# Token-major products 512 columns wide in a two-layer hybrid decoder

## The chip, the cores and the metric

The kernel runs on one core of a Trainium2 chip. The metric is the device time of one execution, in microseconds. Three executions of the kernel before took 2058.93, 2059.01 and 2060.22 us; the median is 2059.01 us.

A core has a matrix engine (TensorE, PE in the profile, with its weight loads as PEld), a vector engine (VectorE, DVE), an engine for pointwise functions (ScalarE, ACT), GpSimd (POOL) and SyncE (SP), which issues DMAs here. TensorE multiplies a stationary operand, loaded ahead, with a moving operand that streams through, and writes to PSUM, where DVE and ACT read it. PSUM is used as eight tiles of 128 partitions by 512 float32 numbers.

## What is computed

Two layers of a decoder over 512 tokens of width 1024, batch 1. Each layer normalizes x, multiplies it by one wide matrix `w_in` and feeds four branches: a short gated convolution, a sparse attention (an indexer scores all earlier tokens, each token attends to its 128 best), a gated linear recurrence over chunks of 64 tokens (HGRN2), and a cross-attention into 256 memory tokens. Each branch is lifted to width 1024, gated, summed and projected; then comes a gated feed-forward block of width 2816.

```python
h = rmsnorm(x, norm_mix)
(a_x, a_b, a_c, d_q, d_k, d_v, i_q, i_k, i_w,
 g_q, g_f, g_i, g_g, m_q, gate_logits) = split_cols(h @ w_in)
y_a = a_b * causal_conv3(a_c * a_x, conv_w)
y_b = dsa_attention(q, k, d_v, iq, ik, iw)       # q, k normed per head; q, k, iq, ik rotated
y_c = rmsnorm(hgrn2_chunkwise(hq, hk, hv, log_f)) * silu(g_g)
y_m = softmax(mq @ mk.T) @ mv                    # mk, mv = split(rmsnorm(mem) @ mem_w_kv)
merged = sum(gates[n] * (branches[n] @ w_lift[n]) for n in range(4))
x = x + merged @ w_out
gate, up = split(rmsnorm(x, norm_ffn) @ ffn_w_up)
x = x + (silu(gate) * up) @ ffn_w_down
```

All of it is float32.

## The kernel before

**Products.** Every large product is made of three matmuls (`mm3`, lines 260 to 262): both operands are split into a high part, rounded to the engine's faster float32 type, and a low remainder, and hi x hi, hi x lo and lo x hi are summed in PSUM. Weights are loaded by `wchunk` (class `Chunk`, line 216 for the DMA, on SP) into `w_raw`, 2048 columns at most, two buffers. ACT copies a part of up to 1024 columns into `w_hi` and DVE subtracts it to give `w_lo` (line 225); of these parts there are three buffers. Both are given a high priority.

Two kinds of products stand on this.

- `features` (line 242) gives a feature-major result: the stationary operand is a 128x128 tile of the weights, the moving one is 512 tokens of the activations. Each matmul is 512 wide. Two such results are in work at a time. Most of the kernel is of this kind.
- `tokens` (line 252) gives a token-major result: the stationary operand is a 128-token tile of the activations, the moving one the weights' columns. A chunk has 256 columns (in one case 200), so each matmul is 256 wide. One token tile is finished over all contraction steps before the next is begun.

`tokens` is used at four places: `mem_kv` (line 417), keys and values of the memory for both layers, at the start; `values` (line 657), the recurrence's values; `projections` (line 820), q, k, v and the indexer's iq, ik, iw of the sparse attention; and `final` (line 1012), the last part of the second layer's down projection, which ends the kernel.

**Projections.** Five chunks, each with a handler that empties the accumulator of a token tile: `c_kv` (k, v, two heads of iq), `c_iq` (four heads of iq), `c_last` (two heads of iq, ik, iw) and `c_q` twice (four heads of q each). A handler copies a group of heads into a tile `unit` (three buffers; k and ik go into `twin`, two buffers), norms q and k per head (`headnorm`), rotates (`rope`), transposes on PE into a PSUM tile `tr` (line 744) and splits the result into qS or iqS (ACT and, line 751, DVE).

**PSUM.** The eight tiles are divided among `mm` (results of `features` and `tokens`, `MM_BUFS` = 3), `tr` (transpositions and small sums, `TR_BUFS` = 3) and `at` (attention scores and the like, `AT_BUFS` = 2).

**Order.** The program is written with generators. A string `EARLY` per layer says in which order steps of the projections (b), the convolution (c), the memory attention (m) and the selection of the 128 best (s, `select`, on DVE) are emitted. Then `lift` of the memory branch is woven with the rest of the selection, and `lift` of the convolution and `values` with `attend`; then comes the recurrence (its logits zf, zq, zg, line 870, and `head`), lifts, the output projection and the feed-forward block. On top of this a planner with a simulated timeline reorders the instructions of each engine: it takes by priority (order of emission, but for what was given a high one) what its model holds ready, so matmuls of different steps interleave. At run time each engine keeps that order.

```python
for c0, n, handle in ((C_DK, 256, c_kv), (C_DK + 256, 256, c_iq), (C_DK + 512, 200, c_last),
                      (C_DQ, 256, c_q(0)), (C_DQ + 256, 256, c_q(1))):
    w = wchunk(w_in[l][:, c0:c0 + n], KD, n)
    for t in range(NT):
        ps = mm_ps()[:, :n]
        tokens(w, h, t, ps)
        handle(ps, t)
    yield
```

Of the kernel before, what the change touches and what calls it, by code (L numbers as in the profile page):

```python
# [12 lines left out]
F32 = mybir.dt.float32  # L13
# [8 lines left out]
P = 128  # L22
# [22 lines left out]
EARLY = ["mmbcmmbmmbsccsmmcsssmsccbmb", "mmbmmbmmcbsccsmmcsssmsccbmb"]  # L45
MM_BUFS = 3
TR_BUFS = 3
# [22 lines left out]
def hybrid_trunk(ctx: ExitStack, tc: tile.TileContext, x, mem, positions, norm_mix, w_in, conv_w,  # L70
# [171 lines left out]
    def features(w, a, js, k0=0, kt=None, pss=None):  # L242
        """Feature-major products of the 128-column tiles js of a chunk."""
# [8 lines left out]
    def tokens(w, a, t, ps, k0=0, kt=None):  # L252
        kt = w.kt if kt is None else kt
        for k in range(k0, k0 + w.kt):
            mm3(ps, pair(a, k, slice(t * P, (t + 1) * P)), w.at(k - k0), k == 0, k == kt - 1)
# [114 lines left out]
    mem_r2, mem_r4 = small(4, name="mem_r2", bufs=1), small(4, name="mem_r4", bufs=1)  # L370

    def mem_in_T():
# [10 lines left out]
        dve.tensor_copy(mem_r4.rearrange("p (a b) -> p a b", b=2), mem_r[:, :, None].to_broadcast([P, 2, 2]))  # L383
        dve.tensor_mul(mem_r2, mem_r4, mem_r4)
# [32 lines left out]
    def mem_kv(l):  # L417
        kv = sp.tile([P, 4, 2, 2, MEM], F32R, name="kv", bufs=1)
        for q in range(2):
            w = wchunk(mem_w_kv[l][:, q * 256:(q + 1) * 256], KD, 256)  # L420
            kus = []
            ms, r = small(4), small(4, "mk_r", 2)
            for t in range(2):
                ps = mm_ps()[:, :256]
                tokens(w, mt, t, ps)
                ku = sp.tile([P, 2, P], F32, name="ku", bufs=3)
                with tc.high_priority(offset=AHEAD):
                    A(ku.rearrange("p a b -> p (a b)"), ps, AF.Copy)
                for j in range(2):
                    sq = sp.tile([P, P], F32, name="mk_sq", bufs=2)  # L430
                    A(sq, ku[:, j, :], AF.Square, scale=P ** -0.5, accum_out=ms[:, 2 * t + j:2 * t + j + 1])
                kus.append(ku)
            dve.tensor_mul(ms, ms, mem_r2)
            rstd_into(r, ms, small, 4)
            dve.tensor_mul(r, r, mem_r4)
            for t in range(2):
                for j in range(2):
                    dve.tensor_scalar(kus[t][:, j, :], kus[t][:, j, :], r[:, 2 * t + j:2 * t + j + 1], None, op0=OP.mult)
            for j in range(2):
                ps = tr_ps()[:, :MEM]  # L440
                for t in range(2):
                    pe.transpose(ps[:, t * P:(t + 1) * P], kus[t][:, j, :], ident)
# [662 lines left out]
```

## Time and profile before

| | |
|---|---|
| Median of three executions | 2059.01 us |
| Span of the profiled execution | 2057.1 us |
| Instructions | 27077, of which 10588 matmuls |
| PE busy | 2046.8 us |
| PEld, DVE, ACT busy | 1731.1, 1270.5, 1017.1 us |
| DMA, mean over the span | 99 GB/s |
| 512-wide matmuls of mm3 (three lines of 2320) | 6960 |
| 256- and 200-wide token-major matmuls | 2016 and 192 |

The span goes from the first to the last of the program's own instructions in the profiled execution; the executions that are timed have no profile, and their median is 1.9 us above that span. Times in the profile are microseconds unless marked ns, and a line L260 is line 260 of the kernel. In the table of groups a row reads: line, engine, operation, written tile <- read tiles, shape, count, busy time, mean duration, and idle time of the engine before it. In the timeline the first number is the start and the second the duration (of all `xN` if several are merged), and a bracket at the end gives the engine's idle time before the instruction and what ended it. Durations of matmuls include their latency and overlap; the distance between two starts is what a matmul costs the engine. In a tile's or a line's view a row gives shortest, median and longest duration in ns, then the first and the last start.

### The profile page before, as it was taken

Reading aid. Unit: us, or ns where it says so; the run is one execution under the profiler, and the core shown is the slowest. Engines: PE = TensorE matmul, PEld = TensorE weight load, DVE = VectorE, ACT = ScalarE, POOL = GpSimd, SP = SyncE. Lnnn points to the kernel's source line nnn. Section 1 sums busy time; section 2 is a strip of 40 time slices with the busy share of each in tenths; the row PEclk is TensorE's granted clock in tenths of the full one; section 3 lists DMA queues with packets and bytes.
Section 4 is the critical chain, followed back from the end, with each engine's and each line's share of the span. In section 5 each row is a group of like instructions: output and inputs, shape, how many; then the busy total and the mean of one; then the engine's idle time right before and its main releaser. Section 6 shows DMA issues by size and latency. Waiting matters only on the chain.

```text
span 2057.1 us, 27077 instructions
## 1 busy us (share of the span) xinstructions
PE 2046.8 (99%) x10588; PEld 1731.1 (84%) x10588; DVE 1270.5 (62%) x2513; ACT 1017.1 (49%) x1836; POOL 9.8 (0%) x33
## 2 busy tenths in 40 slices
PE   8999999999999999999999999999999999999999
PEld 8998988888888888888889898888888888888889
DVE  6779998547676544334457899953766754532542
ACT  7654655856665423223355456576657643322321
POOL 0000000000000000000000000000000000000000
PEclk9999999999999999999999999999999999999999
DMA  7632222212233232232242223321223332322322
GB/s 255 215 95 86 72 89 93 81 53 92 82 113 113 83 102 92 92 114 92 87 154 93 88 75 97 97 66 62 83 82 109 116 102 83 103 93 92 103 72 93
DMA packets 190783, 203.83 MB, mean 99 GB/s; under 512 B 4270, under 2 KB 182528, under 8 KB 190528
## 3 DMA queue, kind: packets, MB, share of 16 engines
q1 hardware_dynamic: 186944, 193.56, 29.2%
q10 hardware_dynamic: 3552, 8.41, 1.1%
q8 instruction: 83, 1.36, 0.3%
q14 instruction: 44, 0.36, 0.1%
q0 software_dynamic: 160, 0.13, 0.0%
HBM read 191.60 MB, written 10.49 MB: 98 GB/s over the span
## 4 chain that ended last, share of the span: by engine, by line
PE 98%; DMA 1%; DVE 0%; ACT 0%; SPq 0%; issue 0%; DVEq 0%; ACTq 0%
PE mm L261 30%; PE mm L260 30%; PE mm L262 30%; PE tr L705 1%; PE tr L699 1%; PE at L676 1%; PE at L675 1%; PE at L927 1%; DMA w_raw<-in_mem_w_kv_dram 1%; PE at L928 0%; PE at L260 0%; PE at L262 0%; PE at L261 0%; PE at L952 0%; PE tr L643 0%; PE tr L744 0%
## 5 line engine op out<-in xcount | busy, mean ns | idle before, releaser
L261 PE MATMUL mm<-h_lo,w_hi 128*128 128x512 f32 x1664 | 652.1, 392 | 0.0
L260 PE MATMUL mm<-h_hi,w_hi 128*128 128x512 f32 x1664 | 651.8, 392 | 0.0
L262 PE MATMUL mm<-h_hi,w_lo 128*128 128x512 f32 x1664 | 649.5, 391 | 0.0
L225 DVE TENSOR_TENSOR w_lo<-w_raw,w_hi 128x1024 fp32r<-128x1024 f32 (+1 forms) x348 | 419.7, 1207 | 350.7 <-ACT w_hi L97 349.5
L97 ACT ACTIVATE w_hi<-w_raw 128x1024 fp32r<-128x1024 f32 (+1 forms) x348 | 363.5, 1046 | 469.6 <-PE mm L261 416.8
L261 PEld LDWEIGHTS mm<-h_lo,w_hi 128*128 128x128 f32 x1664 | 312.6, 188 | 64.9 <-issue 2.5
L262 PEld LDWEIGHTS mm<-h_hi,w_lo 128*128 128x128 f32 x1664 | 312.4, 188 | 65.1 <-issue 1.4
L260 PEld LDWEIGHTS mm<-h_hi,w_hi 128*128 128x128 f32 x1664 | 312.6, 188 | 64.5 <-issue 2.0
L262 PE MATMUL mm<-w_hi,h_lo 128*128 128x256 f32 (+1 forms) x448 | 128.0, 286 | 0.0
L261 PE MATMUL mm<-w_lo,h_hi 128*128 128x256 f32 (+1 forms) x448 | 126.8, 284 | 0.0
L260 PE MATMUL mm<-w_hi,h_hi 128*128 128x256 f32 (+1 forms) x448 | 126.8, 285 | 0.0
L261 PE MATMUL mm<-a_lo,w_hi 128*128 128x512 f32 x272 | 106.1, 390 | 0.0
L260 PE MATMUL mm<-a_hi,w_hi 128*128 128x512 f32 x272 | 105.9, 389 | 0.0
L262 PE MATMUL mm<-a_hi,w_lo 128*128 128x512 f32 x272 | 105.6, 390 | 0.0
L260 PE MATMUL mm<-y_hi,w_hi 128*128 128x512 f32 x256 | 101.3, 397 | 0.0
L262 PE MATMUL mm<-y_hi,w_lo 128*128 128x512 f32 x256 | 100.2, 392 | 0.0
L261 PE MATMUL mm<-y_lo,w_hi 128*128 128x512 f32 x256 | 100.1, 391 | 0.0
L262 PEld LDWEIGHTS mm<-w_hi,h_lo 128*128 128x128 f32 x448 | 85.6, 191 | 1.4 <-issue 0.8
L260 PEld LDWEIGHTS mm<-w_hi,h_hi 128*128 128x128 f32 x448 | 85.2, 191 | 1.2 <-issue 0.8
L261 PEld LDWEIGHTS mm<-w_lo,h_hi 128*128 128x128 f32 x448 | 85.5, 191 | 0.6
L97 ACT ACTIVATE a_hi<-fg 128x512 fp32r<-128x512 f32 x44 | 27.8, 633 | 109.0 <-DVE fg L1054 109.0
L97 ACT ACTIVATE prob<-prob,small 128x128 f32<-128x128 f32 (+3 forms) x128 | 69.2, 555 | 15.2 <-DVE small L688 14.6
(351 smaller groups left out, 3048.6 us busy)
## 6 DMA issues: line engine op xcount, KB each, us to landing
w_raw<-in_w_in_dram SPq DMA_DIRECT2D x72, 1024.0 KB, 5.0
w_raw<-in_ffn_w_up_dram SPq DMA_DIRECT2D x44, 1024.0 KB, 5.1
w_raw<-in_w_lift_dram SPq DMA_DIRECT2D x32, 512.0 KB, 3.4
w_raw<-in_ffn_w_down_dram SPq DMA_DIRECT2D x16, 1024.0 KB, 5.0
w_raw<-in_mem_w_kv_dram SPq DMA_DIRECT2D x8, 1024.0 KB, 5.2
w_raw<-in_w_out_dram SPq DMA_DIRECT2D x8, 1024.0 KB, 4.9
kv<-kv ACTq DMA_DIRECT2D x8, 512.0 KB, 7.4
xT<-x_spill SPq DMA_DIRECT2D x16, 256.0 KB, 5.8
```

The costliest lines, as they stand in the source:

```text
L97: i = act.activation(dst, src, func, **kw)
L225: dve.tensor_sub(lo, raw[:, k:e], f(hi))
L260: pe.matmul(ps, ah, bh, start=first, stop=False)
L261: pe.matmul(ps, ah, bl, start=False, stop=False)
L262: pe.matmul(ps, al, bh, start=False, stop=last)
L675: pe.matmul(ps, q[:, hh, s], k[0][:, :n], start=True, stop=False)
L676: pe.matmul(ps, q[:, hh, s], k[1][:, :n], start=False, stop=True)
L699: pe.transpose(pp[:, (2 * e + i) * P:(2 * e + i + 1) * P], probs[2 * i + e][:, b * P:(b + 1) * P], ident)
L705: pe.matmul(pv[e * HD:(e + 1) * HD, :], vt[:, b, :], pt[:, b, e * 2 * P:(e + 1) * 2 * P], start=b == 0, stop=b == t)
L927: pe.matmul(pa[:, s], z[:, s], cmr[:, s], start=True, stop=True)
```

## The change

All four places that used `tokens` now use `tokens_wide`. It takes a list of weight chunks that follow one another in the contraction (`halves` makes two chunks of 512 rows each), and a list of accumulators, one per token tile. It goes through the parts of the weights, and for each part through all token tiles, so that a part is used up at once and all accumulators (four; two for the memory) stay open until the last part.

- `mem_kv`: the keys of all four heads in one step of 512 columns, the values likewise; the norms of the keys are made for eight columns at once; two stores to DRAM of all heads in place of four of two heads.
- `values`: one step of 512 columns in place of two of 256.
- `projections`: three chunks of 512, 328 and 384 columns. `c_low` has two heads of q, k, v and four heads of iq; `c_last` four heads of iq, ik and iw; `c_q` six heads of q, in groups of four and two. `EARLY` loses two b's per layer.
- `final`: two steps of 512 columns in place of four of 256; in the last step the add and the store are made in two halves per token tile.
- PSUM: `MM_BUFS` 3 to 4, `TR_BUFS` 3 to 2.

```diff
-EARLY = ["mmbcmmbmmbsccsmmcsssmsccbmb", "mmbmmbmmcbsccsmmcsssmsccbmb"]
-MM_BUFS = 3
-TR_BUFS = 3
+EARLY = ["mmbcmmmmbsccsmmcsssmsccmb", "mmbmmmmcbsccsmmcsssmsccmb"]
+MM_BUFS = 4
+TR_BUFS = 2
...
-    def tokens(w, a, t, ps, k0=0, kt=None):
-        kt = w.kt if kt is None else kt
-        for k in range(k0, k0 + w.kt):
-            mm3(ps, pair(a, k, slice(t * P, (t + 1) * P)), w.at(k - k0), k == 0, k == kt - 1)
+    def tokens_wide(ws, a, kt, pss):
+        k0 = 0
+        for w in ws:
+            for ks, _, _ in w.parts:
+                for t, ps in enumerate(pss):
+                    for k in ks:
+                        mm3(ps, pair(a, k0 + k, slice(t * P, (t + 1) * P)), w.at(k), k0 + k == 0, k0 + k == kt - 1)
+            k0 += w.kt
+    def halves(src, n):
+        return [wchunk(src[i * D // 2:(i + 1) * D // 2], KD // 2, n) for i in range(2)]
...
         def values(hv):
-            for q in range(2):
-                w = wchunk(w_in[l][:, C_GI + q * 256:C_GI + (q + 1) * 256], KD, 256)
-                for t in range(NT):
-                    ps = mm_ps()[:, :256]
-                    tokens(w, h, t, ps)
-                    A(hv[:, t, q * 256:(q + 1) * 256], ps, AF.Copy, scale=r_t[:, t:t + 1])
-                yield
+            pss = [mm_ps() for _ in range(NT)]
+            tokens_wide(halves(w_in[l][:, C_GI:C_GI + 512], 512), h, KD, pss)
+            for t, ps in enumerate(pss):
+                A(hv[:, t, :], ps, AF.Copy, scale=r_t[:, t:t + 1])
+            yield
...
+                def q_part(ps, t, c0, heads, h0):
+                    u = unit(ps, t, c0, heads)
+                    headnorm(u, heads, gq_b[l])
+                    rope(u, heads, t)
+                    heads_T(qS, h0, u.rearrange("p a b -> p (a b)"), heads, t)
+                def c_low(ps, t):
+                    A(vt[:, t, :], ps[:, 192:256], AF.Copy, scale=r_t[:, t:t + 1])
+                    twin(ps, t, 128, True, kS)
+                    iq_part(ps, t, 256, 0)
+                    q_part(ps, t, 0, 2, 6)
                 def c_last(ps, t):
-                    A(iw[:, t, :], ps[:, 192:200], AF.Copy, scale=r8_t[:, t:t + 1])
-                    iq_part(ps, t, 0, 2, 6)
-                    twin(ps, t, 128, False, ikS)
+                    A(iw[:, t, :], ps[:, 320:328], AF.Copy, scale=r8_t[:, t:t + 1])
+                    iq_part(ps, t, 0, 4)
+                    twin(ps, t, 256, False, ikS)
+                def c_q(ps, t):
+                    q_part(ps, t, 0, 4, 0)
+                    q_part(ps, t, 256, 2, 4)
...
-                    for c0, n, handle in ((C_DK, 256, c_kv), (C_DK + 256, 256, c_iq), (C_DK + 512, 200, c_last),
-                                          (C_DQ, 256, c_q(0)), (C_DQ + 256, 256, c_q(1))):
-                        w = wchunk(w_in[l][:, c0:c0 + n], KD, n)
-                        for t in range(NT):
-                            ps = mm_ps()[:, :n]
-                            tokens(w, h, t, ps)
+                    for c0, n, handle in ((C_DQ + 384, 512, c_low), (C_IQ + 256, 328, c_last), (C_DQ, 384, c_q)):
+                        pss = [mm_ps()[:, :n] for _ in range(NT)]
+                        tokens_wide(halves(w_in[l][:, c0:c0 + n], n), h, KD, pss)
+                        for t, ps in enumerate(pss):
                             handle(ps, t)
                         yield
...
     def final(x_tok, w2d, a, kt):
-        for m0 in range(0, KD, 2):
-            cols = slice(m0 * P, (m0 + 2) * P)
-            ws = [(k0, wchunk(w2d[k0 * P:min(k0 + 8, kt) * P, cols], min(8, kt - k0), 256)) for k0 in range(0, kt, 8)]
-            for t in range(NT):
-                ps = mm_ps()[:, :256]
-                for k0, w in ws:
-                    tokens(w, a, t, ps, k0, kt)
-                dve.tensor_add(x_tok[:, t, cols], x_tok[:, t, cols], ps)
+        for m0 in range(0, D, 512):
+            cols = slice(m0, m0 + 512)
+            ws = [wchunk(w2d[k0 * P:min(k0 + 4, kt) * P, cols], min(4, kt - k0), 512) for k0 in range(0, kt, 4)]
+            pss = [mm_ps() for _ in range(NT)]
+            tokens_wide(ws, a, kt, pss)
+            for t, ps in enumerate(pss):
+                for c in ([cols] if m0 == 0 else [slice(m0 + e, m0 + e + 256) for e in (0, 256)]):
+                    dve.tensor_add(x_tok[:, t, c], x_tok[:, t, c], ps[:, c.start - m0:c.stop - m0])
```

104 lines of the change are left out of this document (46 added, 58 removed).

## The prediction

> **What bounds the kernel now.** I read the page first: busy shares, slices and the chain that ended last.
>
> ```profile
> PE 2046.8 (99%) x10588; PEld 1731.1 (84%) x10588; DVE 1270.5 (62%) x2513; ACT 1017.1 (49%) x1836; POOL 9.8 (0%) x33
> PE   8999999999999999999999999999999999999999
> DVE  6779998547676544334457899953766754532542
> PEclk9999999999999999999999999999999999999999
> PE 98%; DMA 1%; DVE 0%; ACT 0%; SPq 0%; issue 0%; DVEq 0%; ACTq 0%
> ```
>
> TensorE (PE) is busy in every slice, at full granted clock, and 98% of the chain is its own work. A busy PE need not be at its peak, so the question is whether it waits between matmuls. The table of waits, for PE alone, answers that. Columns: total us, times, longest.
>
> ```profile
> PE tr L160 <- DMA rows<-in_mem_k_norm_dram: 1.9, 1, 1.9
> PE mm L261 <- DVE w_lo L225: 1.3, 2, 0.8
> ```
>
> These are the longest, 3.2 us, and by the slices PE is below nine tenths in the first alone. For some 2040 us it is handed work without a break, so the time is the sum of what its instructions cost back to back. A change pays if it shortens that sum and opens no holes.
>
> **What one matmul costs.** Durations of matmuls overlap in this profile (each is drawn with its latency). The price of one is the distance between starts, in the timeline.
>
> ```profile
> 1984.74 0.39 PE L262 MATMUL mm<-h_hi,w_lo 128*128 128x512 f32 x1
> ...
> 1985.87 0.39 PE L261 MATMUL mm<-h_lo,w_hi 128*128 128x512 f32 x1
> ...
> 1994.48 0.28 PE L260 MATMUL mm<-w_hi,a_hi 128*128 128x256 f32 x1
> ...
> 1996.40 0.28 PE L261 MATMUL mm<-w_lo,a_hi 128*128 128x256 f32 x1
> ```
> ```profile
> 139.05 0.27 PE L260 MATMUL mm<-w_hi,h_hi 128*128 128x200 f32 x1
> ...
> 139.94 0.27 PE L262 MATMUL mm<-w_hi,h_lo 128*128 128x200 f32 x1
> ```
> ```profile
> 218.20 0.34 PE L675 MATMUL at<-ik_hi,iqS 128*128 128x384 f32 x1
> ...
> 218.55 0.28 PE L261 MATMUL mm<-w_lo,h_hi 128*128 128x256 f32 x1
> ```
>
> 512 wide: 5 steps in 1.13 us, 226 to 227 ns. 256 wide: 16 steps in 1.92 us, 120 ns. 200 wide: 8 steps in 0.89 us, 111 to 112 ns. 384 wide: two of them (L675, L676) in 0.35 us, 175 ns. Two 256s cost 240 ns and one 512 costs 227: 13 ns saved per pair. The 200-wide matmul costs nearly as much as a 256, so it is the worst bargain of all.
>
> **The change, part by part.** How many narrow matmuls there are, from the groups kept apart by shape (one line of mm3 each; two more lines with the same count stand beside every one):
>
> ```profile
> L262 PE MATMUL mm<-w_hi,h_lo 128*128 128x256 f32 x384 | 110.1, 287 | 0.0
> L261 PE MATMUL mm<-w_lo,a_hi 128*128 128x256 f32 x160 | 45.1, 285 | 0.1
> L261 PE MATMUL mm<-w_lo,mt_hi 128*128 128x256 f32 x128 | 37.1, 292 | 1.3 <-DVE w_lo L225 1.3
> L262 PE MATMUL mm<-w_hi,h_lo 128*128 128x200 f32 x64 | 17.9, 280 | 0.0
> ```
>
> Three lines each: 1152 + 480 + 384 = 2016 of width 256 and 192 of width 200. At 120 and 112 ns that is 241.9 + 21.5 = 263.4 us.
>
> After: memory keys and values 384 become 192 of 512; values() 384 become 192 of 512; final() 480 become 240 of 512. The projections, 96 matmuls per chunk and layer, become 192 each of 512, 328 and 384 over two layers. In all 816 of 512 (227 ns, 185.2 us), 192 of 384 (175 ns, 33.6 us) and 192 of 328. No row shows 328: it lies between 256 (120) and 384 (175), and 72/128 of the way is 151 ns, 29.0 us (ends 23.0 and 33.6). Sum 247.8 us. **PE work falls by 15.6 us** (11 to 22 with those ends), of which projections give 7.4, final 3.1, memory and values 2.5 each. The transposes stay: five units and two twins per token tile become five units and two twins.
>
> *Weight parts.* A part of w_hi/w_lo is still 1024 columns or less. Now it holds two contraction steps that all four token tiles use, then is dropped, where before both parts of a chunk were held until the last token tile. In final() that hold made PE wait at each column boundary; the chain of waits shows one of three:
>
> ```profile
> 2006.97 1.07 ACT w_hi L97
> 2008.06 1.24 DVE w_lo L225
> ```
>
> A part lasts 24 x 227 = 5.4 us and takes 1.07 + 1.24 us to split, with three buffers, so this wait goes. What it cost:
>
> ```profile
> L262 PE MATMUL mm<-w_hi,a_lo x160: 277/283/283, 1994.7 to 2052.8; 128*128 128x256 f32 x160
> ```
>
> 159 steps of three matmuls took 58.1 us, and at 120 ns they take 57.2. Gain 0.8 us; if the next part comes late instead, nothing. Loads into w_raw: one more per layer for the projections (same bytes), two fewer in final(), all issued on SP, far ahead and on DMA engines that are busy 0.2 to 0.3 (last but one column of the windows below): nothing. The result's store after the first half in final() is one DMA in place of three; it can hold back the next w_raw on SP only until the fourth add, and two raw buffers are ahead of it: nothing, at worst one landing of 5.0 us:
>
> ```profile
> w_raw<-in_ffn_w_down_dram SPq DMA_DIRECT2D x16, 1024.0 KB, 5.0
> ```
>
> *Small work.* A head norm more per token tile (three groups of q heads in place of two), eight in all, each with five instructions on VectorE (DVE) and four on ScalarE (ACT). The longest of them:
>
> ```profile
> L97 ACT ACTIVATE hn_sq<-unit x16: 401/415/419, 214.3 to 1243.7; 128x256 f32<-128x256 f32 x16
> L739 DVE TENSOR_TENSOR unit<-unit,gq x16: 406/424/426, 217.4 to 1255.7; 128x256 f32<-128x256 f32 x16
> ```
>
> So at most 2.1 us on DVE and 1.7 on ACT each. PE isn't waiting for those engines, so nothing now; if the cover is gone it falls under the accumulator rival below. mem_kv's small operations halve: nothing, they are covered by the transposes of x. Its stores become half as many, twice as large; ScalarE waited for one, since the projections' tiles take over its memory:
>
> ```profile
> ACT twin L97 <- DMA kv<-kv: 3.1, 1, 3.1
> ```
>
> PE did not stop for that, and the first twin now comes some 10 us later: nothing, at most 3.1 us.
>
> *The tail.* The last add and store:
>
> ```profile
> 2053.13 0.42 DVE L1020 TENSOR_TENSOR x_tok<-x_tok,mm 128x256 f32<-128x256 f32 x1 [3.17 <-PE mm L262]
> 2045.18 8.73 SPq L1022 DMA_DIRECT2D out_dram<-x_tok  x4
> ```
>
> Afterwards two adds and two stores follow the last matmul: one more add, **+0.4 us** (0.3 to 0.8 with an issue on SP).
>
> *PSUM, 3/3/2 to 4/2/2.* The real unknown. A token tile's accumulator used to fill alone in 24 matmuls, 2.9 us; now four finish together (last 1.4 us apart) and are emptied in a burst. For the projections emptying goes through three `unit` buffers, each held until its head is normed, turned and transposed. One such unit of c_q, before:
>
> ```profile
> 213.77 0.47 ACT L97 ACTIVATE unit<-mm,rstd_t 128x256 f32<-128x256 f32 x1 [1.31 <-PE mm L262]
> ```
> ```profile
> 221.66 0.27 PE L744 MATMUL tr<-ident,unit 128*128 128x128 f32 x1
> ```
> ```profile
> 226.03 0.43 DVE L751 TENSOR_TENSOR qS<-tr,qS 64x256 fp32r<-64x256 f32 x1
> ```
>
> The unit is held 8 us and its transposition buffer 5 us. c_low and c_q now have eight units in one burst: five have to wait, at 8/3 us each, so the last accumulator is free some 13 us after the first and 9 us after the last matmul. Meanwhile two accumulators (tiles 0 and 1) are free early and hold 48 feature matmuls, 10.9 us. So the cover just suffices: 0. It also did so before: the last unit of the old c_q is read very late,
>
> ```profile
> 254.59 0.46 ACT L97 ACTIVATE unit<-mm,rstd_t 128x256 f32<-128x256 f32 x1
> ```
>
> and PE ran lift() on the two accumulators left. I take 0.5 us for each of the four bursts, **+2.0 us**; ends: -0.5 in all (the fourth accumulator helps features()) and, with DVE at its slowest, the rival below.
>
> *Transpositions on two buffers.* In the attention each head group opens up to four `tr` tiles and one for the product with v; with two buffers this chain gets longer, at the far end by every second one of the 20 copies a layer from `tr` into pt with its handover, 1 us each: 10 us a layer.
>
> ```profile
> 435.09 1.58 ACT L97 ACTIVATE pt<-tr 128x512 f32<-128x512 f32 x3
> ```
>
> PE's cover is the next stage's logits, which start before the attention ends:
>
> ```profile
> 427.80 0.39 PE L260 MATMUL mm<-h_hi,w_hi 128*128 128x512 f32 x1
> ```
> ```profile
> 445.77 0.65 PE L705 MATMUL tr<-pt,vt 128*64 128x256 f32 x4
> ```
> ```profile
> 446.54 0.69 DVE L870 TENSOR_TENSOR zf<-mm,rstd 128x512 f32<-128x512 f32 x1 [3.75 <-PE tr L705]
> ```
>
> Four accumulators take 96 of them, 21.8 us, before any must be emptied. With PE 5 us ahead (3.7 us of projections and 1.3 of values a layer), 18 + 5 = 23 us is needed, but the first accumulator is emptied before the attention ends, which gives 5.4 us more. So some 4 us of lengthening is free. I take **0**; ends 0 and 2 x 6 = 12 us.
>
> **Sum.** -15.6 - 0.8 + 0.4 + 2.0 = -14.0 us against the profiled execution's span of 2057.1: 2043.1 us. The median of the three runs, 2059.01, lies 1.9 us above that span; I add the same: **2045 us**.
>
> **The rivals.**
>
> *Accumulators stay occupied (slower).* Place: c_low and c_q, where DVE is nearly full, because select() runs there.
>
> ```profile
> 200.00:250.00 50.00, 45.19 (x115) 1.00 0.22 69
> 250.00:300.00 50.00, 47.31 (x108) 1.00 0.30 95
> ```
>
> ```profile
> 240.16 0.46 ACT L97 ACTIVATE unit<-mm,rstd_t 128x256 f32<-128x256 f32 x1
> ```
> ```profile
> 253.89 0.38 PE L744 MATMUL tr<-ident,unit 128*128 128x128 f32 x2
> ```
>
> With 47 of 50 us taken, this unit waited 14 us for its transposition. Three buffers then give 4.6 us a unit, and the last of eight is read 23 us after the first, 19 us after the last matmul. Less 10.9 us of cover, PE stands 8 us per burst, 12 us if the first is late too. Four bursts add 32 to 48 us to 2059.0 - 16.0: 2075 to 2091; fewer bursts hit give less. It decides from 4.0 us a burst, where the gain without bursts, 15.6 + 0.8 - 0.4 = 16.0 us, is eaten. For it: all four accumulators hang on one handler, which was not so before. Against it: c_low lies ahead of the full stretch, and in c_q PE has had enough other work so far.
>
> *Part of the gain goes to holes.* Half the above in c_q alone, 2 x 4 us, or the attention's 6 to 8 us: 2051 to 2055.
>
> *Width doesn't pay.* If a token-major product cost by its columns (120 ns per 256, thus 240 for 512, 154 for 328, 180 for 384), the new products would take 195.8 + 29.6 + 34.6 = 260.0 us: 3.4 us saved, and 2059.0 - 3.4 - 0.4 + 2.0 = 2057 us, no change. Against it: the 512-wide row above at 227 ns, in the same trace at the same clock. The Trainium skill, "TensorE: Matmul & The Clock Gate", section "Back-to-back issue gap", speaks for this rival: it gives a warm gap of N/2.4 + 2.5 ns, so that by its figure a pair merged saves only 2.5 ns and the whole change, as an estimate from that page, under 3 us. The trace disagrees: 120 and 227 ns are 13 ns above N/2.4, not 2.5.
>
> **How the numbers follow.** Forecast as summed, 2041 to 2051: 0.58. Part of the gain in holes, 2051 to 2055: 0.13. No change (within 0.2%, 4.1 us, about what a measurement here can tell): 0.09, of which 0.03 for width that doesn't pay and the rest for accumulators that cost just the gain. Slower: 0.20, accumulators, of which a quarter ends below 2066. So faster 0.71, same 0.09, slower 0.20. The range goes from 2040 (no hole, 328 at its low end) to 2066, which leaves out 0.05 below and 0.15 above.
>
> **What would show it.** Right: 512-wide token products 227 ns apart, 1008 fewer matmuls, PE's waits still only at the start. Wrong: PE idle with ACT unit or DVE qS as releaser near 110, 240, 1110 and 1230 us; logits waiting for L705; DVE without pause until well after 350 us; a spacing of 240 ns.

## The result, and the profile after

The changed kernel took 2098.09 us (median of four executions, 2095.04 to 2100.00) against 2058.97 beside it: a ratio of 1.0186, 95% interval 1.0173 to 1.0200. It is 39 us slower, outside the range of the prediction and on the other side of it. The profiled execution took 2097.38 us, its span 2095.4, with a mean granted clock of 0.991 (0.999 before). Over 2095 us that difference is, as an estimate, up to 17 us of work at full clock.

The page of the changed kernel: busy shares, the slices of PE, and the chain that ended last.

```profile
PE 2054.1 (98%) x9580; PEld 1689.5 (81%) x9580; DVE 1269.9 (61%) x2539; ACT 1024.2 (49%) x1848; POOL 9.8 (0%) x33
PE   9989999999999999999999998999999999999999
PE 95%; DVE 2%; ACT 2%; DMA 0%; issue 0%; DVEq 0%; SPq 0%; ACTq 0%
```

PE has 1008 matmuls fewer, as forecast, and stands still for 2095.4 - 2054.1 = 41.3 us where it stood still for 10.3. Two slices are below nine tenths, one of them in the middle, where before it was the first alone. The table of waits, for PE (total us, times, longest):

```profile
PE tr L649 <- DVE mprob L647: 12.3, 4, 3.7
PE tr L703 <- ACT prob L97: 3.2, 6, 0.7
PE tr L649 <- DVE iqS L755: 1.8, 1, 1.8
PE mm L269 <- DVE qg_lo L613: 1.5, 2, 0.8
```

L649 is the memory attention's transposition, L703 the sparse attention's. These waits are in small chains that PE used to cover. By stretches of the first layer (columns: busy us of PE, PEld, DVE, ACT, POOL with counts, granted clock, DMA share, GB/s) they lie at three places; the second layer has them again near 1150, 1260 and 1470 us. Before, PE was busy for all of the same three stretches of the first layer.

```profile
140.00:155.00 15.00, 8.39 (x43) 7.42 (x43) 7.50 (x19) 6.38 (x18) 0.00 (x0) 0.80 0.13 35
255.00:275.00 20.00, 13.21 (x55) 9.83 (x56) 19.32 (x61) 11.96 (x33) 0.00 (x0) 0.91 0.17 53
460.00:475.00 15.00, 11.17 (x70) 6.21 (x70) 5.10 (x20) 12.72 (x27) 1.49 (x4) 1.00 0.00 0
```

The first place in the timeline (start, duration, idle time before it in brackets):

```profile
139.10 0.31 PE L269 MATMUL mm<-w_hi,h_hi 128*128 128x328 f32 x1
...
139.41 0.31 PE L271 MATMUL mm<-w_hi,h_lo 128*128 128x328 f32 x1
139.56 0.49 PE L748 MATMUL tr<-ident,unit 128*128 128x128 f32 x3
141.82 0.63 PE L649 MATMUL tr<-ident,mprob 128*128 128x128 f32 x4 [1.78 <-DVE iqS L755]
...
147.47 0.63 PE L649 MATMUL tr<-ident,mprob 128*128 128x128 f32 x4 [2.63 <-DVE mprob L647]
...
149.20 0.41 PE L270 MATMUL at<-mk,qg_hi 128*128 128x256 f32 x1
149.42 0.42 PE L271 MATMUL at<-mk,qg_lo 128*128 128x256 f32 x1
...
152.31 0.64 PE L269 MATMUL mm<-w_hi,h_hi 128*128 128x328 f32 x1 [0.77 <-DVE qg_lo L613]
...
153.02 0.47 PE L271 MATMUL mm<-w_hi,h_lo 128*128 128x328 f32 x1
153.30 0.47 PE L269 MATMUL mm<-w_hi,h_hi 128*128 128x328 f32 x1
```

c_last (328 wide) is broken off at 139.5 after 63 of its 96 matmuls. That is what three token tiles can do with three of the four parts of the weights: the fourth part needs a buffer that the first one keeps until the last token tile has used it (ACT makes the fourth at 155.18). The accumulator for that tile still holds features of the memory attention's second half, which can't be emptied until the first half has let go of `qg_hi` and `qg_lo`. So c_last goes on at 152.31, when qg_lo is written, and between the two PE has nothing but the memory attention's serial chain.

That chain is late because of its third step in the order of emission, the second set of scores. When those scores were finished on PE, and when DVE took them up:

```profile
112.05 0.28 PE L271 MATMUL at<-mk,qg_lo 128*128 128x256 f32 x1
```
```profile
135.40 0.69 DVE L635 TENSOR_REDUCE small<-at 128x2 f32<-128x512 f32 x1
```

The reduction has no idle time before it: DVE reached it 23 us late because it stands behind much of the handlers of c_low in DVE's own order. Before, the handlers of c_kv stood there, a smaller lot, and the same step waited 5 us (in the second layer of the changed kernel it waits from 1117.4 to 1144.9):

```profile
101.69 0.28 PE L262 MATMUL at<-mk,qg_lo 128*128 128x256 f32 x1
```
```profile
107.39 0.69 DVE L629 TENSOR_REDUCE small<-at 128x2 f32<-128x512 f32 x1
```

### The profile page after: what moved, and what is told of

It is laid out like the page before. It is cut to its first block, busy times and chain, and to the rows that moved or that the text cites. A ratio compares the mean times of both kernels' runs of the same rounds, so it can differ in the third digit from the quotient of the medians.

```text
span 2095.4 us, 25113 instructions
## 1 busy us (share of the span) xinstructions
PE 2054.1 (98%) x9580; PEld 1689.5 (81%) x9580; DVE 1269.9 (61%) x2539; ACT 1024.2 (49%) x1848; POOL 9.8 (0%) x33
## 4 chain that ended last, share of the span: by engine, by line
PE 95%; DVE 2%; ACT 2%; DMA 0%; issue 0%; DVEq 0%; SPq 0%; ACTq 0%
PE mm L269 29%; PE mm L270 29%; PE mm L271 29%; PE tr L709 1%; PE tr L703 1%; PE at L680 1%; PE at L679 1%; ACT prob L97 1%; PE at L934 1%; PE at L935 0%; PE at L269 0%; PE tr L649 0%; PE at L959 0%; PE tr L968 0%; PE tr L748 0%; PE at L271 0%
## 5 line engine op out<-in xcount | busy, mean ns | idle before, releaser
L225 DVE TENSOR_TENSOR w_lo<-w_raw,w_hi 128x1024 fp32r<-128x1024 f32 (+2 forms) x350 | 420.7, 1202 | 400.4 <-ACT w_hi L97 399.4
L97 ACT ACTIVATE w_hi<-w_raw 128x1024 fp32r<-128x1024 f32 (+2 forms) x350 | 364.3, 1041 | 476.3 <-PE mm L270 407.9
L270 PE MATMUL mm<-w_lo,h_hi 128*128 128x512 f32 (+2 forms) x256 | 94.0, 368 | 0.5 <-DVE w_lo L225 0.5
L271 PE MATMUL mm<-w_hi,h_lo 128*128 128x512 f32 (+2 forms) x256 | 93.5, 367 | 0.0
L269 PE MATMUL mm<-w_hi,h_hi 128*128 128x512 f32 (+2 forms) x256 | 91.4, 369 | 1.6 <-DVE qg_lo L613 1.5
L97 ACT ACTIVATE gate_e<-gate 128x512 f32<-128x512 f32 x64 | 40.2, 629 | 46.6 <-DVE gate L515 45.9
L1056 DVE TENSOR_TENSOR fg<-mm,rstd 128x512 f32<-128x512 f32 x44 | 30.2, 691 | 52.1 <-PE mm L271 52.1
L515 DVE TENSOR_TENSOR gate<-mm,rstd 128x512 f32<-128x512 f32 x64 | 43.9, 687 | 26.2 <-PE mm L271 26.0
```

The lines of the kernel that those rows point to most:

```text
L97: i = act.activation(dst, src, func, **kw)
L225: dve.tensor_sub(lo, raw[:, k:e], f(hi))
L269: pe.matmul(ps, ah, bh, start=first, stop=False)
L270: pe.matmul(ps, ah, bl, start=False, stop=False)
L271: pe.matmul(ps, al, bh, start=False, stop=last)
L515: dve.tensor_mul(g, ps, r_b)
```

## The experiments

The expectations speak of these theories. A: a held accumulator, and a chain of fixed length from the selection to the end of the sparse attention. B: the rival on record, unit buffers in the bursts. C: two transposition buffers lengthen the sparse attention. D: transposition tiles of one branch queue behind the other's. E: the fourth accumulator disturbs the order. F: the number of transposition buffers, whoever uses them. G: the wide projections alone. H: the order of emission delays the memory attention.

### Which part of the change costs what

*psum_only*: the old kernel with the new split. *proj_old*: the changed kernel with the old projections.

```diff
-MM_BUFS = 3
-TR_BUFS = 3
+MM_BUFS = 4
+TR_BUFS = 2
```

> The kernel before with only the split of PSUM changed, 3/3/2 to 4/2/2; all products as before. Theory A: the chain from the first max to the last product with v stays 273 to 275 us a layer, PE finds no hole: 2057 to 2062 us. Theory B: the same, no bursts here: 2057 to 2062. Theory C: the chain gets 7 to 10 us longer a layer and PE stops at the end of the attention, 2070 to 2080 us.

> The changed kernel with the five old chunks of the projections, their old handlers and the old EARLY; memory keys and values, values, final and the PSUM split 4/2/2 stay changed. Theories A and B (both put the loss in the projections): the gains of the rest remain, 2059.0 - 3.1 - 2.5 - 2.5 - 0.8 + 0.4 = 2050.5 us, between 2048 and 2055. Theory C: the holes at the end of the attention remain, 2064 to 2072 us.

Measured: psum_only 2076.62 us (ratio 1.0085, 1.0068 to 1.0102), proj_old 2075.80 (1.0081, 1.0066 to 1.0096). So in this order of steps the split costs 17.6 us; making memory, values and final wide on top of it gives 0.8, which the intervals don't tell from nothing; the wide projections cost the other 22.3. Theories A and B are wrong on both runs; C has the split's cost about right (in range for psum_only, 4 us too low for proj_old), though, as follows, not its place. *tr2* takes the split apart: two transposition buffers, still three accumulators.

```diff
-TR_BUFS = 3
+TR_BUFS = 2
```

> The kernel before with two transposition buffers in place of three and still three mm accumulators; one PSUM tile is left unused. Theory D (from psum_only: tr tiles are handed out in the order of emission, so with two of them the transpositions of c_last queue behind the tiles of the memory attention, whose chain has some 15 us per step): c_last's last transposition comes at 180 to 190 us in place of 157, and the time is that of psum_only, 2072 to 2080 us. Theory E (the fourth mm accumulator lets products of the convolution run ahead of c_last and of the logits): without it nothing changes, 2057 to 2062 us.

2079.73 us (1.0097, 1.0083 to 1.0111): the missing third transposition buffer is the whole cost of the split, and the fourth accumulator, if anything, gives back 3 us. Part of where it goes shows in the last four transpositions of c_last's `twin` (duration ns, then first and last start), before, in tr2, in psum_only and after:

```profile
L766 PE MATMUL tr<-ident,twin x4: 272/272/273, 145.7 to 157.0; 128*128 128x128 f32 x4
```
```profile
L766 PE MATMUL tr<-ident,twin x4: 270/272/273, 162.0 to 178.1; 128*128 128x128 f32 x4
```
```profile
L766 PE MATMUL tr<-ident,twin x4: 271/272/272, 166.9 to 187.9; 128*128 128x128 f32 x4
```
```profile
L770 PE MATMUL tr<-ident,twin x4: 270/272/273, 168.3 to 187.8; 128*128 128x128 f32 x4
```

With the same handlers a token tile takes 3.8 us before (a third of 157.0 - 145.7) and 5.4 to 7 with two buffers, and the selection, which needs all four, starts later: its first maximum comes at 172.9 us before, 191.2 in tr2 and 201.4 in psum_only. In the changed kernel it takes 6.5, but c_last has four heads of iq there in place of two, and with three buffers (wide_332 below) it still takes 5.8. In tr2 and psum_only some of the cost also comes from the start of the kernel, where the memory's keys are transposed; in tr2:

```profile
PE mm L260 <- ACT ku L97: 6.1, 2, 5.3
```

Does the sparse attention itself get longer with two buffers, as theory C says? From the last mask of the selection (L818, L827) to the last product with v (L705, L709), before and after:

```profile
L818 DVE TENSOR_SCALAR bias<-score x3: 286/362/419, 205.4 to 340.9; 128x256 f32<-128x256 f32 x1, 128x384 f32<-128x384 f32 x1, 128x512 f32<-128x512 f32 x1
...
L705 PE MATMUL tr<-pt,vt x80: 379/379/431, 358.5 to 446.0; 128*64 128x256 f32 x80
```
```profile
L827 DVE TENSOR_SCALAR bias<-score x3: 294/360/423, 234.8 to 369.1; 128x256 f32<-128x256 f32 x1, 128x384 f32<-128x384 f32 x1, 128x512 f32<-128x512 f32 x1
...
L709 PE MATMUL tr<-pt,vt x80: 379/379/431, 387.8 to 475.1; 128*64 128x256 f32 x80
```

105.1 and 106.0 us; with only the split changed, in psum_only, it is 101.0 (365.7 to 466.7). No: the attention is as long as it was, but in the changed kernel it ends 29 us later, and PE, which has run ahead with the logits as far as its accumulators allow, meets the bare end of it (the third stretch above).

*own_narrow* and *own_wide* give the memory attention and the projections a transposition tile each, in psum_only and in the changed kernel; all others alternate.

```diff
-    def tr_ps():
-        return pat.tile([P, 512], F32, name="tr", bufs=TR_BUFS)
+    def tr_ps(name=None):
+        turn[0] += name is None
+        return pat.tile([P, 512], F32, name=name or ("tr", "tu")[turn[0] % 2], bufs=1)
...
-                    pm = tr_ps()
+                    pm = tr_ps("tr")
...
-                    ps = tr_ps()[:, :heads * HD]
+                    ps = tr_ps("tu")[:, :heads * HD]
```

> The kernel before with the split 4/2/2, as in psum_only, but the two transposition tiles kept apart: one for the memory attention, one for unit and twin of the projections; all other users take them in turn. Nothing can then queue behind the other branch's tiles, though each has but one. Theory D: c_last's transpositions follow its matmuls again and end before 170 us, the first max is before 185 us, the time falls from 2076.6 to 2060 to 2068 us. Theory E: no change against psum_only, 2074 to 2080 us. Theory C (the attention's own transpositions are short of buffers): no change or slower, since these still have two.

> The changed kernel with the same separation of the two transposition tiles, nothing else. Theory D: c_last's transpositions no longer wait for the memory attention; the hole at 140 us (an accumulator held by the features of the memory attention) stays, some 11 us a layer, the later ones shrink: 2075 to 2090 us. Theory E or C: 2094 to 2102 us.

2092.74 and 2112.00 us, both slower than with the shared pair. Theory D, that one branch's tiles queue behind the other's, forecast a gain and got none; but each branch now has one tile in place of two shared ones, so the runs don't tell queueing from having fewer. With one buffer, c_last's transpositions follow each other at 12 us a token tile; for own_narrow, their weight loads:

```profile
L769 PEld LDWEIGHTS tu<-ident,twin x4: 140/140/142, 179.1 to 215.9; 128*128 128x128 f32 x4
```

So the number of buffers matters; a handler's tile is free again only when ACT and DVE have both read it. And in own_wide, where the memory attention has its own tile, DVE takes up its second scores, finished on PE at 111.5, no sooner:

```profile
142.87 0.69 DVE L638 TENSOR_REDUCE small<-at 128x2 f32<-128x512 f32 x1
```

### The hole at 140 us

*late_m6* moves the memory attention's second features behind c_last.

```diff
-EARLY = ["mmbcmmmmbsccsmmcsssmsccmb", "mmbmmmmcbsccsmmcsssmsccmb"]
+EARLY = ["mmbcmmmbmsccsmmcsssmsccmb", "mmbmmmcbmsccsmmcsssmsccmb"]
```

> The changed kernel, with the features of the memory attention's second half emitted behind c_last instead of ahead of it (EARLY mmbcmmmbms... and mmbmmmcbms...), nothing else. Theory A (a held accumulator plus a long chain): these features hold one of the four accumulators until the first half's attention has let go of qg_hi and qg_lo, c_last cannot finish without it, so PE's hole at 139.8 to 152.3 us (and near 1150 to 1200) goes, 11 us a layer; the selection starts some 11 us earlier, the chain from the first max of the selection to the last product with v stays 273 to 275 us, and part of the later holes goes too: 2062 to 2078 us. Theory B (the rival on record: unit buffers in the bursts of c_low and c_q): these are untouched, 2094 to 2100 us. Theory C (two buffers for transpositions lengthen the attention): the holes at 460 to 474 stay at 7 us a layer, and the hole at 140 is not explained.

2091.65 us (1.0159, 1.0144 to 1.0174). The hole goes, as theory A says, but only 6.4 us of the 22 come back: c_last's matmuls now run from 118.9 to 135.2, yet its transpositions start at 175.94, right behind the memory attention's fourth set:

```profile
175.51 0.60 PE L649 MATMUL tr<-ident,mprob 128*128 128x128 f32 x4
175.94 0.38 PE L748 MATMUL tr<-ident,unit 128*128 128x128 f32 x2
```

The late chain was moved from in front of c_last's matmuls to in front of its handlers. *between* changes where the chain becomes late: the handlers of c_low are emitted between the steps of the memory attention. *between_late* does this and late_m6's move.

```diff
                         for t, ps in enumerate(pss):
                             handle(ps, t)
-                        yield
+                            yield
...
-EARLY = ["mmbcmmmmbsccsmmcsssmsccmb", "mmbmmmmcbsccsmmcsssmsccmb"]
+EARLY = ["mmbmbmbbcmmbbbbsccsmmcsssmsccmbbbb", "mmbmbmbbmmcbbbbsccsmmcsssmsccmbbbb"]
```

> The changed kernel, with the handlers of c_low's four token tiles emitted between the memory attention's third and fourth step and not all ahead of them (the matmuls stay where they were). Theory H (tiles of tr are handed out in the order of emission, so the memory attention's third step, and with it everything behind it, waits until c_low's burst of twelve transpositions, 112 to 139.6 us, has drained): the second set of the memory attention's transpositions starts before 128 us in place of 141.8, PE's hole at 140 to 152 us shrinks to under 4 us, and the time falls by 10 to 25 us, 2073 to 2088. Theory F (the number of buffers, whatever the order): the second set stays after 138 us, 2094 to 2102 us.

> As the run before this one, and the features of the memory attention's second half behind c_last as in late_m6. Theory H: the hole at 140 goes for the same reason; c_last is no longer held by an accumulator either, its last transposition comes before 180 us: 2070 to 2086 us. Theory F: 2088 to 2100 us, as late_m6.

2084.50 (1.0121, 1.0104 to 1.0137) and 2084.07 us (1.0119, 1.0104 to 1.0134): 13.6 and 14.0 us less than the changed kernel, as theory H expects; its second set of transpositions starts at 120.3 in *between* (in between_late c_last's last transposition comes at 181.9, a little later than expected). DVE there takes up the second scores 0.3 us after PE has finished them, and the first of the three stretches is full again, while the other two shrink only (PE stands 5.9 and 1.9 us where it stood 7.0 and 3.8):

```profile
110.41 0.69 DVE L635 TENSOR_REDUCE small<-at 128x2 f32<-128x512 f32 x1 [0.33 <-PE at L271]
```
```profile
140.00:155.00 15.00, 14.82 (x90) 13.45 (x90) 13.39 (x56) 11.95 (x35) 0.00 (x0) 1.00 0.41 128
...
250.00:275.00 25.00, 19.14 (x77) 14.02 (x77) 23.58 (x77) 13.91 (x39) 0.00 (x0) 0.86 0.12 40
460.00:475.00 15.00, 13.14 (x68) 7.95 (x69) 6.45 (x17) 10.84 (x23) 1.49 (x4) 0.89 0.00 1
```

In the first layer the new string also puts a step of the convolution behind two of the memory's. In the second it doesn't, and there the stop goes as well: from 1150 to 1175 us PE is busy for 25.00 of 25 us, against 20.50 in the changed kernel. But theory H named the wrong thing that is ordered. Of the 30 us from the scores (112.05) to their transposition (141.82), 23 pass in DVE's queue and under 2 are a wait for the transposition tile; in own_wide, with a tile of its own, the step was as late.

*mem_late* emits c_low and c_last ahead of the whole memory attention.

```diff
-EARLY = ["mmbcmmmmbsccsmmcsssmsccmb", "mmbmmmmcbsccsmmcsssmsccmb"]
+EARLY = ["bcbmmmmmcsmcsmmcsssmsccmb", "bcbmmmmmcsmcsmmcsssmsccmb"]
```

> The changed kernel with c_low and c_last emitted ahead of the whole memory attention (EARLY bcbmmmmmcsmcsmm... in both layers). No memory step can then hold an accumulator or a transposition buffer that c_last needs. Theory F: c_last's matmuls follow c_low's without PE's hole at 140, its last transposition comes at 155 to 170 us and the first max of the selection before 180; holes come later if at all, where the memory attention now ends: 2070 to 2090 us. Theory B (unit buffers): c_low's eight units still drain over some 30 us, c_last's after them, last transposition after 175 us, 2090 us or more.

2115.00 us (1.0271, 1.0256 to 1.0285), the slowest of all. c_last's last transposition came at 158.8, as early as before, and yet the selection's first maximum came at 243.0, against 201.4 in the changed kernel: the indexer's first product starts right behind the memory attention's fourth step, which is now the late one.

```profile
218.46 0.60 PE L649 MATMUL tr<-ident,mprob 128*128 128x128 f32 x4
...
223.07 0.28 PE L679 MATMUL at<-ik_hi,iqS 128*128 128x256 f32 x1
```

Theory F has the transpositions right, and the selection's start and the time wrong. By this the selection hangs on two chains, c_last's handlers and the memory attention's first half; the old order kept both short by alternating small lots of them. That is read from the order in these traces; no run tests it by itself.

### What sets the pace of the burst

After its last matmul at 105 us, c_low takes 34 us until its last transposition at 139.6. *unit_more* has four unit buffers in place of three, *hn2* two for the squares of a head norm in place of one, *wide_332* three transposition buffers, with the fourth accumulator from `at`.

```diff
-                    u = ip.tile([P, 4, HD], F32, name="unit", bufs=3)[:, :heads]
+                    u = ip.tile([P, 4, HD], F32, name="unit", bufs=4)[:, :heads]
```
```diff
-                    sq = ip.tile([P, 4, HD], F32, name="hn_sq", bufs=1)[:, :heads]
+                    sq = ip.tile([P, 4, HD], F32, name="hn_sq", bufs=2)[:, :heads]
```
```diff
-MM_BUFS = 4
-TR_BUFS = 2
+MM_BUFS = 3
+TR_BUFS = 3
...
-                        pss = [mm_ps()[:, :n] for _ in range(NT)]
+                        pss = [mm_ps()[:, :n] for _ in range(NT - 1)] + [at_ps()[:, :n]]
```

> The changed kernel with four unit buffers in place of three (more do not fit beside the rest). Theory B (the rival on record: the bursts drain at a third of a unit's hold): they drain a quarter faster, c_low's 27 us become some 20, 2085 to 2094 us. Theory F (transposition buffers set the pace): no change, 2095 to 2101 us.

> The changed kernel with two buffers for hn_sq, the squares of a head norm, in place of one. If this single buffer sets the pace at which c_low drains (its norms follow one another, two per token tile), the drain of 34 us after its last matmul (105 to 139.6) falls below 28 us and the time by 5 to 15 us, 2083 to 2093; if the pace comes from the hand-overs between ACT and DVE in one unit's chain, nothing changes, 2095 to 2101 us.

> The changed kernel with the old split of PSUM, 3/3/2: the three mm accumulators serve token tiles 0 to 2 and one tile of at serves tile 3, in projections, values and final. Theory F (two transposition buffers cost some 20 us in any kernel, since each transposition holds its buffer some 5 us until ACT and DVE have both read it; the wide projections cost the rest): c_last's last transposition comes 10 to 20 us earlier than the 187.8 us of the changed kernel, 2073 to 2085 us. Theory G (the loss is in the wide projections alone, whose accumulators wait for one another): 2092 us or more, as an at tile is now held through a burst too.

2101.33, 2099.77 and 2097.16 us: nothing gained, and the burst ends at 139.8, 141.4 and 139.2. So it isn't the unit buffers (theory B falls), nor the squares, nor the transposition buffers. What is left is the hand-overs in each unit's own chain and the places that the engines' orders give them; that is argued, not shown. The longest waits of ACT and DVE between 105 and 140 us in the changed kernel stand behind transpositions on PE, which is never idle there:

```profile
ACT iqS L97 <- PE tr L748: 6.9, 3, 5.5
DVE iqS L755 <- ACT iqS L97: 3.8, 1, 3.8
```

DVE finishes a unit at 121.96, and PE transposes it at 125.08, behind products of the convolution.

wide_332 came out as theory G has it, not F: c_last's last transposition comes at 184.1 us, 3.7 us earlier and not 10 to 20. The stretch at the end of the attention is full (25.00 of 25 us from 450 to 475), but PE stops elsewhere, above all between 200 and 250 (42.87 of 50 us). That the tiles of `at` held as accumulators cause this is argued, not shown. Its longest waits:

```profile
PE tr L649 <- DVE mprob L647: 16.7, 6, 3.9
PE at L269 <- ACT mpt_hi L97: 6.4, 9, 0.7
```

*between_332* is wide_332 with the order of between_late.

```diff
-EARLY = ["mmbcmmmmbsccsmmcsssmsccmb", "mmbmmmmcbsccsmmcsssmsccmb"]
+EARLY = ["mmbmbmbbcmbbbbmsccsmmcsssmsccmbbbb", "mmbmbmbbmcbbbbmsccsmmcsssmsccmbbbb"]
```

> wide_332 (all products wide, PSUM 3/3/2, the fourth accumulator from at) with the order of between_late: c_low's handlers between the steps of the memory attention, the features of its second half behind c_last. Theory H (order) together with F (buffers): the hole at 140 us goes as it did in between_late, and the one at 460 as it did in wide_332; what stays is PE's standing at 200 to 275 us, 10 to 16 us a layer: 2070 to 2084 us. If the two causes are one and the same, no more than wide_332 or between_late gave: 2084 us or more.

2094.82 us (1.0173, 1.0159 to 1.0187), outside the 2070 to 2084 expected: the two remedies don't add up. From 140 to 155 us PE is busy for 9.98 of 15, now waiting for DVE inside the handlers, and the granted clock is 0.66. Why is open.

### A later c_last without wide products

*last_late* is the old kernel with c_last two convolution steps later.

```diff
-EARLY = ["mmbcmmbmmbsccsmmcsssmsccbmb", "mmbmmbmmcbsccsmmcsssmsccbmb"]
+EARLY = ["mmbcmmbmmccbssmmcsssmsccbmb", "mmbmmbmmcccbssmmcsssmsccbmb"]
```

> The kernel before (narrow products, 3/3/2) with the chunk c_last emitted two steps of the convolution later in both layers, some 22 us of PE's work (96 matmuls at 227 ns); no step is added or taken away. Theory A: the first max of the selection comes 20 to 24 us later, the chain of 273.5 us keeps its length, and its end is later by as much; once PE has used up the work that does not hang on it (6 to 18 us of it) it stands: 4 to 16 us a layer, 2067 to 2091 us, with holes at the last steps of the memory attention or the end of the attention. Theories B and C: accumulators, bursts and buffers are those of before, 2057 to 2062 us.

2074.83 us (1.0076, 1.0061 to 1.0091). The size is theory A's, the place isn't: the end of the attention moved by 7 us only, and PE stops at 200 to 250, where the convolution used to cover c_q (45.93 of 50 us, against 50.00). Its stop there is for a unit:

```profile
PE mm L260 <- ACT unit L97: 2.8, 1, 2.8
```

So no chain of fixed length from the selection's start to the attention's end, which theory A claimed, exists: here it was 14 us shorter. What the run shows is that PE has next to no spare work in this part of the layer: 96 matmuls moved forward are missing where they were cover.

### The other places one by one

*edges* makes only the memory's keys and values and the last down projection wide, on 3/3/2; *final_only* only the latter; *final_values* the latter and the values. The fourth accumulator of final and values is a tile of `at`.

```diff
-            pss = [mm_ps() for _ in range(NT)]
+            pss = [mm_ps() for _ in range(NT - 1)] + [at_ps()]
             tokens_wide(ws, a, kt, pss)
```

> The kernel before with PSUM 3/3/2 and only those two of the four places made wide that lie away from the attention: the memory's keys and values (two accumulators) and the last down projection (three mm accumulators and one of at, which is idle there). If the prediction's terms for these were right, 2059.0 - 2.5 - 3.1 - 0.8 + 0.4 = 2053.0 us, between 2051 and 2056. If every wide product loses by its burst, 2059 or more.

> The kernel before with the last down projection alone made wide, on PSUM 3/3/2, the fourth accumulator from at. From the run with the memory's keys and values wide as well, where the start lost 5.3 us and the end gained 4.2: 2054.5 to 2056 us, faster than both kernels. If the 1.1 us by which that run's span exceeded the one of before are noise of both parts: 2057 to 2060 us.

> As final_only (PSUM 3/3/2, the last down projection wide), with the recurrence's values wide as well, three mm accumulators and one of at. In wide_332, where values are made in the same way on three transposition buffers, PE found no hole at the end of the attention. If the term of the prediction holds (2.5 us for both layers), 2056.2 - 2.5 = 2053.7 us, between 2052 and 2055; if an at tile held through the attention costs as much as it gives, 2056 to 2060 us.

final_only took 2056.17 us against 2059.44 beside it, a ratio of 0.9984 (0.9975 to 0.9993): faster than both kernels. edges took 2059.11 (0.9999, 0.9990 to 1.0007) and final_values 2059.10 (1.0000, 0.9991 to 1.0009), so the wide memory products and the wide values each cost 2.9 us against final_only where 2.5 were to be gained. They lose in two ways. In edges PE stands for 10.7 us in all, hardly more than the 10.2 of final_only; what differs is the clock. Behind the memory's products PE stops for 1.9 and 0.9 us at 81 to 85, and then runs at half clock until about 95 (before, then edges; the third number from the end is the granted clock):

```profile
50.00:100.00 50.00, 49.87 (x358) 46.65 (x357) 36.88 (x149) 32.57 (x87) 1.19 (x4) 1.00 0.69 226
```
```profile
50.00:100.00 50.00, 47.19 (x267) 42.25 (x266) 35.31 (x140) 32.88 (x83) 1.19 (x4) 0.90 0.58 210
```

Over the whole kernel the mean granted clock is 0.995 or 0.996 in all eleven runs of edges and 0.998 or 0.999 in those of final_only, which is, as an estimate, some 5 us of 2058. In final_values the clock is that of final_only, and PE stands 3.5 us longer, 1.8 and 1.7 in the two layers' attentions (400 to 450 and 1400 to 1450 us); it waits there for what it had been covering:

```profile
PE tr L711 <- ACT prob L97: 2.2, 2, 1.1
```

A tile of `at` is held there as well, so that final_values doesn't tell the burst from the missing `at` tile.

## Why the prediction was wrong

- *What one matmul costs*: right. 512-wide token-major matmuls follow each other at 227 ns, 384-wide at 173 to 174 (medians), and the 328-wide of the timeline above (139.10 to 139.41, two steps) at 155, with a median of 151. So the rival that width doesn't pay is out, and PE's work fell as summed. It rose again where it was drawn out: PE's busy time is 7.3 us longer with 15.6 us less to do, from matmuls at half clock (up to 17 us by the estimate above) and ends in front of stops. The prediction has no term for the clock.
- *Weight parts, tail, final()*: right in their sum. Terms of -3.1, -0.8 and +0.4 make -3.5; final_only measured -3.3.
- *Memory and values*, -2.5 each: the work fell, but each lost 5.4 elsewhere. The step that failed is the tacit one that a wide product costs nothing around it outside the projections: the memory's cost some 5 us of clock, and the values' 3.5 us of standing, to which the tile of `at` may have added.
- *Transpositions on two buffers*, taken at 0, ends 0 and 12: the main failure: the split alone cost 17.6 us (psum_only) and two transposition buffers alone 20.4 (tr2). The text looked at one user of these buffers, the sparse attention, and got that one right (105.1 and 106.0 us). It didn't count the others: the handlers of c_last, which gate the selection, and the memory's keys at the start.
- *Small work*, "PE isn't waiting for those engines, so nothing now": failed. The handlers' order on DVE holds up the memory attention by 23 us, which no count of busy time shows; emitting them between its steps took 13.6 us off the time (between).
- *Accumulators*, 0.5 us for each of four bursts, and the rival with 8 to 12: the rival had c_low as a place and about the price of one burst (6.6 us of standing at 140, and some 2 more at half clock), but its mechanism, unit buffers and PE waiting for accumulators they keep, is wrong. One more unit buffer did nothing; the accumulator PE waited for belonged to the memory attention. c_q, its other place, showed no stop of its own.
- *What would show it*: of the signs named, PE idle with a unit or qS as releaser near 110 and 240 didn't appear, DVE working until well after 350 did (last mask 369.1, 340.9 before), and the logits met the end of the attention.
- *The chances*: the classes, from 2041 us up, add up to 1.00 already, so the 0.05 put below 2040 has no place among them.

By runs the 39 us are 17.6 for the split, -0.8 for the three small places on it, 22.3 for the wide projections, of which 13.6 went with the order of emission alone (between). These shares hold for this order of steps only: wide_332 has three transposition buffers and is as slow as the changed kernel. The other 8.7 stay unassigned: in between_332 the stop at 460 is gone and most of that at 255 (22.90 of 25 us from 250 to 275), but PE stands at 140, and between 200 and 250 (46.17 of 50 us), instead.

## What to carry to other kernels

When the bound engine is busy by 99%, ask what covers each serial chain, and how much cover is left, before pricing what the engine saves: a product that ends in one burst moves small work, in the order in which an engine gets it, in front of other chains, and here two chains that were 23 and 28 us late, one a layer, cost 13.6 us, nearly all of the 15.6 that 1008 fewer matmuls were to save. Count the clock too: short stops were followed by half clock. For a buffer that is taken away, list every user of its pool, not the one that looks most loaded. Among the places tried apart here, the wide form paid at the kernel's end alone, where little else hung on the old product.

## What the runs showed that was not expected

After the stops of the first stretch the granted clock was 0.50, from 149.2 to 155.8 us: the 328-wide matmuls from 152.31 to 155.5 follow each other at 273 to 274 ns (153.02 to 153.30 above), then at some 150. PE had stood for 1.8, 0.7, 2.6 and 0.8 us, together 5.9 of the 8.8 us from 140.0 to 148.8; the 256-wide steps had slowed by 149.2 already (0.22 us to the next start, 120 ns before), within the memory attention's products. The Trainium skill, "TensorE: Matmul & The Clock Gate", Part 1, gives half the clock after an idle window of about 3.4 us; no single stop here was that long, so in this trace several short ones were enough. Its section "Back-to-back issue gap" gives N/1.2 for a cold array, 273 ns for 328, and the trace agrees. The warm formula that the prediction takes from that section is given there for an isolated matmul; for a stream with weight loads the section has about 131 ns at 512 wide, where this trace has 227.

The cost of a late chain is not its own length. In the runs whose selection began 18 to 31 us later than before (tr2, last_late, psum_only, between and the changed kernel) the time grew by 8 to 20 us a layer, other causes included.
